# A hybrid decoder layer on one core: decay and rate products together, retention by alternating heads, all weight sums of the last two down parts by DMA, another order of the last products

## The chip, the cores and the metric

The kernel runs on one core of a Trainium2 chip. The time is that of one execution on the device, in microseconds (us). A core has a matrix engine (TensorE, PE in the profile), a vector engine (VectorE, DVE), a scalar engine (ScalarE, ACT), GpSimd (POOL), and SyncE (SP), which here does nothing but start DMA transfers. Each engine works off its own list of instructions in a fixed order; engines wait for each other by semaphores.

## What is computed

One layer of a decoder on 512 tokens of width 2048, all in float32. RMSNorm, a token mixer of four head groups that run side by side, an output projection, RMSNorm, an MLP with squared ReLU, a final RMSNorm:

```python
a = rmsnorm(x, norm1_w)
p_gdn, p_ret, p_m2, p_rw = split(a @ w_in)
o = concat([gated_deltanet(p_gdn), retention(p_ret), mamba2(p_m2), rwkv7(p_rw)])
h = x + o @ w_out
h = h + square(relu(rmsnorm(h, norm2_w) @ w_up)) @ w_down
out = rmsnorm(h, final_norm_w)
```

The change touches two of the head groups. Retention, per head and chunk, is `scores = (q k^T) * dmask`, `o = scores v + (q * qdec) R`, with a state `R` that is carried from chunk to chunk. RWKV-7 needs a decay, `exp(-exp(-softplus(-(w0 + tanh(wl) @ w_up)) - 0.5))`, and a rate, `a = sigmoid(a0 + al @ a_up)`; both come from small products with 32 rows.

## The kernel before

**Precision.** Each weight slab (128x1024) is split into a high part (`hi`, a cast on ACT) and a low part (`lo`, `raw - hi` on DVE); a product is three matmuls, hi by hi, hi by lo, lo by hi. Matmuls with plain float32 operands, as in the head groups, go through PE in two passes, and the trace lists each pass as a row.

**Token mixing.** `ORDER` lists 12 units: four of RWKV (`rwkv(j)`, "D"), four of gated DeltaNet ("A"), two of Mamba-2 ("C"), and last two of retention (`ret(j)`, "B"; each has two heads, `hh` = 0 and 1, in rows 0 to 63 and 64 to 127). Each unit first takes its parts of the input projection (`proj()`, line 457, 48 matmuls of 128x512 a part); the rest of a unit runs as a generator that is advanced by `tick()` once for every four matmuls of a later projection, so that its small matmuls lie between large ones. PE and POOL execute in exactly the order in which the code is written; the instructions of DVE, ACT and SP are put into an order by a scheduler when the kernel is built, and keep it. PSUM banks for small products come from a ring of six (`BK()`).

**MLP.** Both products of the MLP use Strassen-Winograd's scheme: seven products (numbered `m` = 1 to 7) in place of eight, with sums of weight blocks as operands. `up` runs from about 1076 to 1737 us, `down` from there to the end. `down` has eight parts `c`; each has two halves of columns `s`, in each the seven products in the order `DORD[c]`, and in each of them two slabs `i` (`dslab` counts the slabs) of 12 matmuls. `down_ahead` makes the splits of up to three slabs ahead of PE; there are four buffers each for `hi` and `lo`. Row blocks `t` = 0 and 1 have their results in `ht[t]`, those of tokens 256 to 511 in `ht[2 + t]`; a block of 128 tokens is finished by products 3, 2 (tokens 0 to 255) or 7, 4 (the others).

**Sums of weights.** Four of the seven weight operands in `down` are sums of blocks. Those of products 5 and 7 are made in DRAM beforehand: `add_weights` copies one block into a DRAM tile `t` by a DMA from POOL (line 313) and adds the other in an accumulating DMA one step later (lines 315, 318). A step is sent off by `add_one` after each of 52 projections, and after every seventh of the 216 products of `up` (`u % 7 == 4`); before each stands a `pace` copy on ACT and a multiplication on POOL. There were 64 steps. The sums of products 6 and 4 are made on DVE at the time of their split (line 1572), from the loaded sum of product 5 and the blocks of products 3 and 2 (`SUM`); `USES` says how many splits use a loaded slab.

**The end.** In part 7 each product is followed by the additions into `ht`; `finish` sends squares to ACT (line 377, summed along the row) and multiplies by the final norm's weights on DVE (line 1708); `write` takes the sum of squares to the power -0.5 on POOL (line 374), scales the four tiles of 128x512 of a row block (odd ones on ACT, line 1717, even ones on DVE, line 1719) and writes them out (line 1720).

Of the kernel before, what the change touches and what calls it, by code (L numbers as in the profile page):

```python
# [191 lines left out]
def tile_trunk(ctx: ExitStack, tc: tile.TileContext, ins, out):  # L192
# [104 lines left out]
        return ins["wdn"][4 * c + 2 * i + q, 2 * j + s]  # L297

    sums = {}

    def add_weights():

        late = None
        for c in range(8):
            for s in range(2):
                for q in range(2):
                    for m, y in ((5, wd(c, 0, 0, s, q)), (7, wd(c, 1, 1, s, q))):
                        h = yield
                        pace = cp.tile([128, 2], F32, tag="pace", name="pace", bufs=8)
                        A.copy(pace[:, 0:1], h[:, 0:1].bitcast(F32))  # L310
                        G.tensor_tensor(pace[:, 1:2], pace[:, 0:1], mhalf[:, 0:1], op=ALU.mult)  # L311
# [261 lines left out]
    def rwkv(j):  # L573
# [5 lines left out]

        bk = BK()  # L580
        PE.matmul(bk, lora[0:32, 512 + 128 * j:640 + 128 * j], m1[0:32], start=True, stop=True)
        sw = S("sw")
        A.activation(sw, bk, AF.Tanh, scale=0.5, bias=hb[:, j:j + 1])
        V.tensor_scalar(sw, sw, 1.0, None, op0=ALU.add)
        cs = S("cs")
        V.tensor_tensor_scan(cs, C("reset"), sw, 0.0, ALU.mult, ALU.add)
# [5 lines left out]
        V.tensor_copy(gc, gn[:, :, 63])  # L592
        k = shift((yield from proj()), Pm("mu", 4 + j), omu[:, 6 + j:7 + j])

        bk = BK()
        PE.matmul(bk, lora[96:128, cols], m0[96:128], start=True, stop=True)
        a = S("a")
        A.activation(a, bk, AF.Tanh, scale=0.5, bias=hb[:, 4 + j:5 + j])
        V.tensor_scalar(a, a, 0.5, 0.5, op0=ALU.mult, op1=ALU.add)
        kr = S("kr")  # L600
        V.tensor_scalar(kr, k, Pm("kk", j), None, op0=ALU.mult)
# [504 lines left out]
    def ret(j):  # L1106
        swap = [i ^ 1 for i in range(32)]

        def rot(acc):
            q = S("rq")  # L1110
            A.copy(q, acc)
            r = S("rr")
            V.tensor_tensor(r, q, C("cos"), op=ALU.mult)
            V.stream_shuffle(q, q, swap)
            V.tensor_tensor(q, q, C("sin"), op=ALU.mult)
            V.tensor_tensor(r, r, q, op=ALU.add)
            return r

        half = (slice(0, 64), slice(64, 128))
        qr = q4(rot((yield from proj())))  # L1120
        qd = q4(S("qd"))
        V.tensor_tensor(qd, qr, bc(C("qdec", 128 * j, 128).unsqueeze(1), (128, 4, 128)), op=ALU.mult)
        kf = rot((yield from proj()))
        kr = q4(kf)
        v0, v1 = S("rv0"), S("rv1")
        A.copy(v0, (yield from proj()))
        kd = S("kd").rearrange("p (c h d) -> p c h d", c=4, h=2)
        bk = tposes(None, kf)
        V.tensor_tensor(kd, bk.rearrange("p c (h d) -> p c h d", h=2),
                        bc(C("kdec", 2 * j, 2).unsqueeze(1).unsqueeze(3), (128, 4, 2, 64)), op=ALU.mult)  # L1130
        vt = [q4(S("vt0")), q4(S("vt1"))]
        PT = [q4(S("PT0")), q4(S("PT1"))]

        def scores(hh):
            bk = q4(BK())
            for c in range(4):
                PE.matmul(bk[:, c], kr[half[hh], c], qr[half[hh], c], start=True, stop=True)
            V.tensor_tensor(PT[hh], bk, bc(C("dmask", 128 * (2 * j + hh), 128).unsqueeze(1), (128, 4, 128)), op=ALU.mult)

        A.copy(v1, (yield from proj()))  # L1140
        tposes(vt[0], v0)
        scores(0)
        zg = [S("zg0"), S("zg1")]
        silu2(q4(zg[0]), (yield from proj()))
        tposes(vt[1], v1)
        scores(1)
        sb = q4(BK("sb"))
        R = q4(S("R"))
        for hh in range(2):
            for c in range(3):  # L1150
                PE.matmul(sb[half[hh], c], kd[:, c, hh], vt[hh][:, c], start=True, stop=True)
        V.tensor_copy(R[:, 0], sb[:, 0])
        for c in (1, 2):
            V.scalar_tensor_tensor(R[:, c], R[:, c - 1], C("rdec", j, 1), sb[:, c], op0=ALU.mult, op1=ALU.add)
        silu2(q4(zg[1]), (yield from proj()))
        yield "P"
        ocs = []
        for hh in range(2):
            ob = q4(BK("ob"))
            for c in range(4):  # L1160
                PE.matmul(ob[:, c], PT[hh][:, c], vt[hh][:, c], start=True, stop=c == 0)
                if c > 0:
                    PE.matmul(ob[:, c], qd[half[hh], c], R[half[hh], c - 1], start=False, stop=True)
            mu4, va, rs = small("mu4", 4), small("va", 4), small("rs", 4)
            V.tensor_reduce(mu4, ob, axis=AX.X, op=ALU.add)
            V.tensor_scalar(mu4, mu4, 1.0 / 128, None, op0=ALU.mult)
            oc = q4(S("oc"))
            V.tensor_tensor(oc, ob, bc(mu4.unsqueeze(2), (128, 4, 128)), op=ALU.subtract)
            sq = q4(S("sq"))
            A.activation(sq, oc, AF.Square)  # L1170
            V.tensor_reduce(va, sq, axis=AX.X, op=ALU.add)
            V.tensor_scalar(va, va, 1.0 / 128, EPS, op0=ALU.mult, op1=ALU.add)
            rsqrt(rs, va, 4)
            V.tensor_tensor(oc, oc, bc(rs.unsqueeze(2), (128, 4, 128)), op=ALU.mult)
            ocs.append(oc)
            yield 3
        yield 8
        for hh in range(2):
            bk = q4(BK())
            for c in range(4):  # L1180
                PE.transpose(bk[:, c], ocs[hh][:, c], ident)
            o = S("oB")
            V.scalar_tensor_tensor(q4(o), bk, hn[:, 1 + 2 * j + hh:2 + 2 * j + hh], q4(zg[hh]), op0=ALU.mult, op1=ALU.mult)
            keep_o(4 + 2 * j + hh, o)
# [310 lines left out]


    DPROD = {1: 2, 2: 1, 3: 0, 4: 4, 5: 6, 6: 7, 7: 5}
    DORD = [(1, 5, 6, 3, 2, 4, 7)] * 7 + [(1, 5, 6, 3, 2, 7, 4)]
    SUM = {6: (5, 3), 4: (5, 2)}
    USES = {1: 1, 5: 3, 3: 2, 2: 2, 7: 1}  # L1500
    dseq, dslab, dh, dop, dr = [], {}, {}, {}, {}
# [27 lines left out]
    def down_load():  # L1529

        if ds["l"] >= len(dseq):
            return False
        e = dseq[ds["l"]]
        if e[0] == "w":
            _, c, s, m, i = e
            m = SUM[m][1] if m in SUM else m
            e = ("w", c, s, m, i)
        if e in dr:
            ds["l"] += 1
            return True  # L1540
        n = len(homes["raw"])
        if len(ring) >= n and ring[-n][0] > 0:
            return False
        if e[0] == "x":
            src, uses = hq[e[1]][:, DPROD[e[2]]].rearrange("p k t -> p (k t)"), 1
        else:
            src = sums[m, c, s, i] if m in (5, 7) else wd(c, m != 1, m == 3, s, i)
            uses = USES[m]
        r = new_raw()
        nc.sync.dma_start(r, src)  # L1550
        dr[e] = [uses, r]
        ring.append(dr[e])
        ds["l"] += 1
        return True

    def down_ahead(i):

        while ds["s"] < len(dseq):
            e = dseq[ds["s"]]
            if e[0] == "w" and dslab[e[1:]] > i + 3:  # L1560
                break
            while ds["l"] <= ds["s"]:
                assert down_load()
            if e[0] == "x":
                both = AT("x").rearrange("p a t -> p (a t)")
                h, l = dop[e[1:]] = both[:, :1024], both[:, 1024:]
            else:
                h, l = dh[e[1:]] = new_halves()
            if e[0] == "w" and e[3] in SUM:
                _, c, s, m, q = e  # L1570
                r, other = (dr["w", c, s, x, q] for x in SUM[m])
                V.tensor_tensor(r[1], r[1], other[1], op=ALU.add)  # L1572
                other[0] -= 1
            else:
                r = dr[e]
            A.copy(h, r[1])  # L1576
            V.tensor_tensor(l, r[1], h.bitcast(F32), op=ALU.subtract)  # L1577
            r[0] -= 1
            ds["s"] += 1
        while ds["l"] < ds["s"] + 5 and down_load():  # L1580
            pass
# [128 lines left out]
    def write(t):  # L1710
# [2 lines left out]
        V.tensor_scalar(s1[:, 0:1], s1[:, 0:1], 1.0 / D, EPS, op0=ALU.mult, op1=ALU.add)  # L1713
        rsqrt(s1[:, 1:2], s1[:, 0:1], 1)
        for i in range(4):
            if i % 2:
                A.activation(ht[t][i], ht[t][i], AF.Copy, scale=s1[:, 1:2])
            else:
                V.tensor_scalar(ht[t][i], ht[t][i], s1[:, 1:2], None, op0=ALU.mult)
            (nc.sync, nc.scalar)[i % 2].dma_start(out[0, 128 * t:128 * t + 128, 512 * i:512 * i + 512], ht[t][i])  # L1720

    c = 7
# [49 lines left out]
```

## Time and profile before

| what | value |
|---|---|
| median of 3 runs | 2349.72 us (2349.24 to 2351.58) |
| the profiled execution, its own time | 2356.37 us |
| its span in the trace | 2354.6 us |
| mean granted PE clock | 0.992 |
| PE busy | 2290.2 us (97%) |
| DVE busy | 1772.2 us (75%) |
| ACT busy | 1016.7 us (43%) |
| POOL busy | 194.8 us (8%) |
| DMA | 404.76 MB, mean 172 GB/s |

Times in the trace are counted from the start of the span. PE is busy nearly all the time, so a stretch gets shorter where PE gets less to do or waits less. A row of the timeline has the start, the duration, the engine, the line, the operation, what it writes and reads, and in brackets the time that the engine stood idle before it and what ended that. Matmuls overlap, so what a run of them costs is read from start to start.

### The profile page before, as it was taken

What the parts mean: (1) busy time and instruction counts of PE and PEld (TensorE: products, weight loads), DVE (VectorE), ACT (ScalarE), POOL (GpSimd) and SP (SyncE); (2) the same over time, 40 slices, a digit from 0 to 9 for tenths busy, and PEclk for the clock granted to TensorE, in tenths of its full rate; (3) what the DMA queues carried; (4) which work ended last, traced back from release to release, by engine and by line L of the source; (5) the groups of instructions that cost most, each with busy time, mean ns of one, the idle gap of its engine ahead of it and who ended that gap; (6) DMA issues with size and microseconds to landing.
All of it is one profiled execution on the core that took longest, in us unless ns stands there. A gap on an engine that the chain in (4) does not pass through costs nothing.

```text
span 2354.6 us, 36711 instructions
## 1 busy us (share of the span) xinstructions
PE 2290.2 (97%) x14690; PEld 1969.7 (84%) x14690; DVE 1772.2 (75%) x2783; ACT 1016.7 (43%) x1480; POOL 194.8 (8%) x270
## 2 busy tenths in 40 slices
PE   6999999999999999998999999999999999999996
PEld 6777778878776788878999999999988888888885
DVE  5686855765684544469888888888888988898898
ACT  5323233333322232355455555555565444444443
POOL 1110211211111210011111000000010000000000
PEclk9999999999999999999999999999999999999998
DMA  5553625745553757565877754445486555656451
GB/s 201 148 144 90 170 78 147 182 123 143 153 153 95 196 151 243 154 227 175 243 221 206 218 172 137 158 157 169 149 312 199 196 185 163 215 172 213 157 192 72
DMA packets 159915, 404.76 MB, mean 172 GB/s; under 512 B 12928, under 2 KB 79488, under 8 KB 158720
## 3 DMA queue, kind: packets, MB, share of 16 engines
q1 hardware_dynamic: 83952, 285.42, 37.2%
q0 software_dynamic: 38912, 77.08, 14.5%
q10 hardware_dynamic: 36880, 39.92, 4.9%
q8 instruction: 115, 1.88, 0.3%
q14 instruction: 56, 0.46, 0.1%
HBM read 355.70 MB, written 113.77 MB: 199 GB/s over the span
## 4 chain that ended last, share of the span: by engine, by line
PE 78%; DVE 10%; issue 6%; DMA 4%; POOL 1%; ACT 1%; SPq 0%; POOLq 0%; DVEq 0%; ACTq 0%
PE acc L457 16%; PE p L1443 8%; PE p L1445 8%; PE p L1444 8%; PE dn L1677 8%; PE dn L1678 8%; PE dn L1676 8%; PE wo L1241 2%; PE wo L1242 2%; PE wo L1249 2%; DVE lo L282 1%; PE acc L481 1%; DMA h<-ct 1%; DVE lo L1577 1%; DVE xi L567 1%
## 5 line engine op out<-in xcount | busy, mean ns | idle before, releaser
L1576 ACT CAST hi<-raw 128x1024 fp32r<-128x1024 f32 x224 | 235.3, 1055 | 291.6 <-PE dn L1678 228.2
L1676 PE MATMUL dn<-hi,x 128*128 128x512 f32 x896 | 349.6, 390 | 5.6 <-ACT hi L1576 5.6
L1677 PE MATMUL dn<-lo,x 128*128 128x512 f32 x896 | 349.8, 390 | 3.2 <-DVE lo L1577 3.1
L1678 PE MATMUL dn<-hi,x 128*128 128x512 f32 x896 | 349.3, 390 | 0.0
L281 ACT CAST hi<-raw 128x1024 fp32r<-128x1024 f32 x162 | 169.7, 1049 | 401.6 <-PE acc L457 297.9
L457 PE MATMUL acc<-ah,hi 128*128 128x512 f32 x832 | 336.5, 404 | 0.0
L457 PE MATMUL acc<-al,hi 128*128 128x512 f32 x832 | 335.5, 403 | 0.0
L457 PE MATMUL acc<-ah,lo 128*128 128x512 f32 x832 | 333.8, 401 | 0.0
L1577 DVE TENSOR_TENSOR lo<-raw,hi 128x1024 fp32r<-128x1024 f32 x224 | 272.7, 1222 | 62.8 <-ACT hi L1576 62.4
L1436 ACT CAST hi<-raw 128x1024 fp32r<-128x1024 f32 x216 | 226.5, 1051 | 208.9 <-PE p L1444 149.3
L1437 DVE TENSOR_TENSOR lo<-raw,hi 128x1024 fp32r<-128x1024 f32 x216 | 262.7, 1221 | 70.7 <-ACT hi L1436 70.3
L282 DVE TENSOR_TENSOR lo<-raw,hi 128x1024 fp32r<-128x1024 f32 x160 | 195.2, 1222 | 141.1 <-ACT hi L281 124.9
L1676 PEld LDWEIGHTS dn<-hi,x 128*128 128x128 f32 x896 | 168.7, 188 | 41.5 <-ACT hi L1576 6.5
L1677 PEld LDWEIGHTS dn<-lo,x 128*128 128x128 f32 x896 | 168.6, 188 | 39.8 <-DVE lo L1577 4.9
L1678 PEld LDWEIGHTS dn<-hi,x 128*128 128x128 f32 x896 | 168.7, 188 | 34.8
L457 PEld LDWEIGHTS acc<-ah,hi 128*128 128x128 f32 x832 | 156.7, 188 | 38.5 <-issue 7.4
L457 PEld LDWEIGHTS acc<-ah,lo 128*128 128x128 f32 x832 | 156.7, 188 | 34.3 <-issue 2.9
L457 PEld LDWEIGHTS acc<-al,hi 128*128 128x128 f32 x832 | 156.9, 189 | 31.8 <-issue 1.9
L1434 DVE TENSOR_TENSOR raw<-raw,raw 128x1024 f32<-128x1024 f32 x124 | 151.4, 1221 | 2.2 <-DMA raw<-in_wup_dram 0.5
L1572 DVE TENSOR_TENSOR raw<-raw 128x1024 f32<-128x1024 f32 x64 | 77.7, 1221 | 0.6
L311 POOL TENSOR_TENSOR pace<-pace,mhalf 128x1 f32<-128x1 f32 x64 | 39.5, 618 | 443.6 <-ACT pace L310 443.6
L1445 PE MATMUL p<-s2h,lo 128*128 128x256 f32 x256 | 72.5, 283 | 0.8 <-DVE lo L1437 0.8
(500 smaller groups left out, 5008.0 us busy)
## 6 DMA issues: line engine op xcount, KB each, us to landing
raw<-in_wup_dram SPq DMA_DIRECT2D x136, 512.0 KB, 5.7
t<-in_wdn_dram POOLq DMA_DIRECT2D x128, 512.0 KB, 8.1
raw<-in_win_dram SPq DMA_DIRECT2D x106, 512.0 KB, 3.9
raw<-in_wdn_dram SPq DMA_DIRECT2D x96, 512.0 KB, 4.5
h<-ct ACTq DMA_DIRECT2D x32, 1024.0 KB, 10.1
raw<-t SPq DMA_DIRECT2D x64, 512.0 KB, 4.4
raw<-h SPq DMA_DIRECT2D x56, 512.0 KB, 4.3
raw<-in_wout_dram SPq DMA_DIRECT2D x48, 512.0 KB, 3.7
```

What stands on the lines that cost most here:

```text
L282: by.tensor_tensor(l[:, :w], r[:, :w], h[:, :w].bitcast(F32), op=ALU.subtract)
L457: PE.matmul(acc[:w], a, b, start=n == 0, stop=n == 47)
L1436: A.copy(h, r)
L1437: V.tensor_tensor(l, r, h.bitcast(F32), op=ALU.subtract)
L1443: PE.matmul(acc, wh, rh[:, k], start=k == 0, stop=False)
L1444: PE.matmul(acc, wh, rl[:, k], start=False, stop=False)
L1445: PE.matmul(acc, wl, rh[:, k], start=False, stop=k == 7)
L1576: A.copy(h, r[1])
L1577: V.tensor_tensor(l, r[1], h.bitcast(F32), op=ALU.subtract)
L1676: PE.matmul(accs[t], xh, h[:, ws], start=kk == 0, stop=False)
L1677: PE.matmul(accs[t], xh, l[:, ws], start=False, stop=False)
L1678: PE.matmul(accs[t], xl, h[:, ws], start=False, stop=kk == 3)
```

## The change

There are five edits.

1. In `rwkv`, the product for the rate stands right behind that for the decay, with its activation, instead of one projection later.
2. In `ret`, the scores of both heads are made in one go (`scores()`), head by head in turn, into two banks; the states alternate between the heads too, and so do the outputs, which had been one head after the other, with three ticks between.
3. `add_weights` also makes the sums of products 6 and 4 for parts 6 and 7 (`LATE = 6`): product 6 from a block and the sum of product 5, product 4 from a block and the sum of product 6. These are 16 more steps, 80 in all.
4. For those parts `down` loads one slab per product and does no additions on DVE.
5. In part 7 product 7 comes fourth instead of sixth, and `write` scales all tiles of row blocks 0 and 1 on ACT.

```diff
-                    for m, y in ((5, wd(c, 0, 0, s, q)), (7, wd(c, 1, 1, s, q))):
+                    parts = [(5, wd(c, 0, 1, s, q), wd(c, 0, 0, s, q)), (7, wd(c, 0, 1, s, q), wd(c, 1, 1, s, q))]
+                    if c >= LATE:
+                        parts += [(6, wd(c, 1, 1, s, q), 5), (4, wd(c, 1, 0, s, q), 6)]
+                    for m, x, y in parts:
...
-                        G.dma_start(d, wd(c, 0, 1, s, q))
+                        G.dma_start(d, x)
                         if late:
                             G.dma_start(*late, accum_op=ALU.add, max_dma_last_dim=1024)
-                        late = d, y
+                        late = d, (sums[y, c, s, q] if y in (5, 6) else y)
...
         PE.matmul(bk, lora[0:32, 512 + 128 * j:640 + 128 * j], m1[0:32], start=True, stop=True)
+        ba = BK()
+        PE.matmul(ba, lora[96:128, cols], m0[96:128], start=True, stop=True)
         sw = S("sw")
         A.activation(sw, bk, AF.Tanh, scale=0.5, bias=hb[:, j:j + 1])
+        a = S("a")
+        A.activation(a, ba, AF.Tanh, scale=0.5, bias=hb[:, 4 + j:5 + j])
...
-        bk = BK()
-        PE.matmul(bk, lora[96:128, cols], m0[96:128], start=True, stop=True)
-        a = S("a")
-        A.activation(a, bk, AF.Tanh, scale=0.5, bias=hb[:, 4 + j:5 + j])
...
-        def scores(hh):
-            bk = q4(BK())
+        def scores():
+            bks = [q4(BK()), q4(BK())]
             for c in range(4):
-                PE.matmul(bk[:, c], kr[half[hh], c], qr[half[hh], c], start=True, stop=True)
-            V.tensor_tensor(PT[hh], bk, bc(C("dmask", 128 * (2 * j + hh), 128).unsqueeze(1), (128, 4, 128)), op=ALU.mult)
+                for hh in range(2):
+                    PE.matmul(bks[hh][:, c], kr[half[hh], c], qr[half[hh], c], start=True, stop=True)
+            for hh in range(2):
+                V.tensor_tensor(PT[hh], bks[hh], bc(C("dmask", 128 * (2 * j + hh), 128).unsqueeze(1), (128, 4, 128)), op=ALU.mult)
...
-        for hh in range(2):
-            for c in range(3):
+        for c in range(3):
+            for hh in range(2):
                 PE.matmul(sb[half[hh], c], kd[:, c, hh], vt[hh][:, c], start=True, stop=True)
...
+        obs = [q4(BK("ob")), q4(BK("ob"))]
+        for c in range(4):
+            for hh in range(2):
+                PE.matmul(obs[hh][:, c], PT[hh][:, c], vt[hh][:, c], start=True, stop=c == 0)
+            for hh in range(2 if c > 0 else 0):
+                PE.matmul(obs[hh][:, c], qd[half[hh], c], R[half[hh], c - 1], start=False, stop=True)
         for hh in range(2):
-            ob = q4(BK("ob"))
-            for c in range(4):
-                PE.matmul(ob[:, c], PT[hh][:, c], vt[hh][:, c], start=True, stop=c == 0)
-                if c > 0:
-                    PE.matmul(ob[:, c], qd[half[hh], c], R[half[hh], c - 1], start=False, stop=True)
+            ob = obs[hh]
...
-    DORD = [(1, 5, 6, 3, 2, 4, 7)] * 7 + [(1, 5, 6, 3, 2, 7, 4)]
+    DORD = [(1, 5, 6, 3, 2, 4, 7)] * 7 + [(1, 5, 6, 7, 3, 2, 4)]
...
-            m = SUM[m][1] if m in SUM else m
+            m = SUM[m][1] if m in SUM and c < LATE else m
...
-            src = sums[m, c, s, i] if m in (5, 7) else wd(c, m != 1, m == 3, s, i)
-            uses = USES[m]
+            src = sums[m, c, s, i] if (m, c, s, i) in sums else wd(c, m != 1, m == 3, s, i)
+            uses = USES[m] if c < LATE else 1
...
-            if e[0] == "w" and e[3] in SUM:
+            if e[0] == "w" and e[3] in SUM and e[1] < LATE:
...
-            if i % 2:
+            if i % 2 or t < 2:
                 A.activation(ht[t][i], ht[t][i], AF.Copy, scale=s1[:, 1:2])
```

What this makes of the lists of instructions is shown at three places. The first is PE's list in the first retention unit, from the transposes of `v1` on (`rv`), with `vt`, `PT` and the state `R` as above. Before:

```order
L1004 MATMUL bk<-ident,rv_7171 128x128 x4
L1137 MATMUL bk<-rr 128x128 x4
L1151 MATMUL sb<-vt_7388,kd 64x128 x3
L1151 MATMUL sb<-vt_7389,kd 64x128 x3
```

and, one projection later, the outputs of its first head:

```order
L1161 MATMUL ob<-vt_7388,PT_7390 128x128 x2
L1163 MATMUL ob<-R,qd 128x128
L1161 MATMUL ob<-vt_7388,PT_7390 128x128
L1163 MATMUL ob<-R,qd 128x128
L1161 MATMUL ob<-vt_7388,PT_7390 128x128
L1163 MATMUL ob<-R,qd 128x128
```

Now the scores of both heads stand one projection earlier, and the outputs of both heads in one block:

```order
L1166 MATMUL ob<-vt_7388,PT_7390 128x128
L1166 MATMUL ob<-vt_7389,PT_7391 128x128
L1166 MATMUL ob<-vt_7388,PT_7390 128x128
L1166 MATMUL ob<-vt_7389,PT_7391 128x128
L1168 MATMUL ob<-R,qd 128x128 x2
L1166 MATMUL ob<-vt_7388,PT_7390 128x128
L1166 MATMUL ob<-vt_7389,PT_7391 128x128
L1168 MATMUL ob<-R,qd 128x128 x2
```

The second block of the other head, three ticks later, is gone, and consecutive matmuls are now of different heads.

The second place is the end of ACT's list. The tiles are named after the column block, `h_1` is the second, and a number: before, 17645 to 17648 are row block 0, the next four row block 1, then 2, then 3. Before, the last rows were these:

```order
L1576 CAST hi<-raw 128x1024
L377 ACTIVATE junk,fss<-h_3_17656 128x512
L377 ACTIVATE junk,fss<-h_3_17660 128x512
L377 ACTIVATE junk,fss<-h_1_17654 128x512
L377 ACTIVATE junk,fss<-h_1_17658 128x512
L1717 ACTIVATE h_1_17654<-h_1_17654,s_22443 128x512
L1717 ACTIVATE h_3_17656<-h_3_17656,s_22443 128x512
```

Now 17741 to 17744 are row block 0, and so on, and the end of ACT's list reads (between the fences two more scalings and the issues of writes are left out):

```order
L381 ACTIVATE junk,fss<-h_1_17750 128x512
L1724 ACTIVATE h_0_17741<-h_0_17741,s_22497 128x512
L1724 ACTIVATE h_1_17742<-h_1_17742,s_22497 128x512
L1724 ACTIVATE h_2_17743<-h_2_17743,s_22497 128x512
```

```order
L1724 ACTIVATE h_3_17748<-h_3_17748,s_22513 128x512
L1724 ACTIVATE h_1_17750<-h_1_17750,s_22555 128x512
L1727 DMA out_dram<-h_3_17748 128x512
L1727 DMA out_dram<-h_1_17750 128x512
L1724 ACTIVATE h_3_17752<-h_3_17752,s_22555 128x512
L381 ACTIVATE junk,fss<-h_1_17754 128x512
```

The square of the last tile of row block 3 (`h_1_17754`) now stands behind the eight scalings of row blocks 0 and 1 and two of row block 2; before, all squares stood ahead of the scalings of row blocks 2 and 3, and one cast stood behind the scalings of row blocks 0 and 1.

The third place is DVE's list at the end. Now (`fw` are the final norm's weights, `s` the scale of a row block):

```order
L1687 TENSOR_TENSOR h_1_17742<-h_1_17742,dn 128x512
L1687 TENSOR_TENSOR h_1_17746<-h_1_17746,dn 128x512
L1687 TENSOR_TENSOR h_1_17750<-h_1_17750,dn 128x512
L1715 TENSOR_TENSOR h_1_17742<-h_1_17742,fw 128x512
L1719 TENSOR_REDUCE s_22497<-fss 128x1
L1715 TENSOR_TENSOR h_1_17746<-h_1_17746,fw 128x512
L1720 TENSOR_SCALAR s_22497<-s_22497 128x1
```

Before, the last sum of a weight slab and the scalings of row blocks 0 and 1 stood ahead of product 7's additions:

```order
L1572 TENSOR_TENSOR raw<-raw 128x1024
L1719 TENSOR_SCALAR h_0_17645<-h_0_17645,s_22340 128x512
L1719 TENSOR_SCALAR h_2_17647<-h_2_17647,s_22340 128x512
L1713 TENSOR_SCALAR s_22356<-s_22356 128x1
L1680 TENSOR_TENSOR m_17643<-m_17643,dn 128x512
```

The sums of slabs are gone from DVE's list, and the addition from the last product (`h_1_17750`, row block 2) now stands ahead of the first scale of row block 0.

More of the change, by code (lines that the diff above doesn't have):

```diff
@@ L299, in tile_trunk @@
     sums = {}
+    LATE = 6
     def add_weights():
@@ L1132, in ret @@
         PT = [q4(S("PT0")), q4(S("PT1"))]
-        def scores(hh):
-            bk = q4(BK())
+        def scores():
+            bks = [q4(BK()), q4(BK())]
             for c in range(4):
-                PE.matmul(bk[:, c], kr[half[hh], c], qr[half[hh], c], start=True, stop=True)
-            V.tensor_tensor(PT[hh], bk, bc(C("dmask", 128 * (2 * j + hh), 128).unsqueeze(1), (128, 4, 128)), op=ALU.mult)
+                for hh in range(2):
+                    PE.matmul(bks[hh][:, c], kr[half[hh], c], qr[half[hh], c], start=True, stop=True)
+            for hh in range(2):
+                V.tensor_tensor(PT[hh], bks[hh], bc(C("dmask", 128 * (2 * j + hh), 128).unsqueeze(1), (128, 4, 128)), op=ALU.mult)
         A.copy(v1, (yield from proj()))
         tposes(vt[0], v0)
-        scores(0)
+        scores()
         zg = [S("zg0"), S("zg1")]
@@ L1145, in ret @@
         tposes(vt[1], v1)
-        scores(1)
         sb = q4(BK("sb"))
         R = q4(S("R"))
-        for hh in range(2):
-            for c in range(3):
+        for c in range(3):
+            for hh in range(2):
                 PE.matmul(sb[half[hh], c], kd[:, c, hh], vt[hh][:, c], start=True, stop=True)
```

## The prediction

> **What bounds the kernel now.** I read the busy times by stretch first (start and end, length, then busy us of PE, PEld, DVE, ACT, POOL with counts, granted clock, DMA share, GB/s).
>
> ```profile
> 64.00:760.00 696.00, 685.93 (x4893) 531.65 (x4892) 473.40 (x1226) 222.42 (x415) 105.98 (x139) 1.00 0.53 136
> 1170.00:1400.00 230.00, 230.00 (x1931) 230.00 (x1932) 192.84 (x232) 124.22 (x182) 20.71 (x28) 1.00 0.70 209
> 1400.00:1737.00 337.00, 337.00 (x2769) 334.39 (x2768) 278.08 (x336) 183.09 (x258) 0.00 (x0) 1.00 0.49 162
> 2127.00:2203.00 76.00, 76.00 (x337) 62.96 (x336) 66.67 (x71) 35.26 (x34) 0.00 (x0) 1.00 0.57 187
> 2260.00:2300.00 40.00, 40.00 (x178) 33.15 (x177) 39.70 (x53) 18.39 (x29) 0.00 (x0) 1.00 0.37 120
> 2300.00:2344.00 44.00, 35.88 (x144) 27.62 (x142) 41.38 (x61) 18.16 (x30) 2.08 (x2) 0.92 0.13 48
> ```
>
> PE has no idle time in `up` and in nearly all of `down`: there only less PE work would help, and the change takes none. In the last 44 us PE is busy for 35.88 while DVE is full from 2260 on: the end of part 7 is bound by DVE. So two places can gain: small matmuls in the token mixing, and the end.
>
> **The rate's product.** The timeline of PE around the decay's product (`m,lora`, 32 rows) in the first unit:
>
> ```profile
> 64.75 0.39 PE L457 MATMUL acc<-ah,lo 128*128 128x512 f32 x1
> 65.07 1.12 PE L581 MATMUL bk<-m,lora 32*128 32x512 f32 x2
> 66.12 0.50 PE L457 MATMUL acc<-ah,hi 128*128 128x512 f32 x1
> 66.46 0.40 PE L457 MATMUL acc<-al,hi 128*128 128x512 f32 x1
> 66.69 0.39 PE L457 MATMUL acc<-ah,lo 128*128 128x512 f32 x1
> ```
>
> Three large matmuls in a row take 3 x 0.227 = 0.68 us from start to start (last rows: 0.23 each). Here 66.69 - 64.75 = 1.94, so the two passes cost 1.26: about 0.85 for the passes and 0.4 for the change of shape before and after. The rate's product costs the same 13 us later. Put behind the decay's, it uses rows 96 to 127 of the array, which the other leaves free, and another bank. Whether such neighbours run at once shows in the same shapes elsewhere:
>
> ```profile
> 104.05 1.16 PE L664 MATMUL bk<-AR,KB 64*128 64x128 f32 x16
> 105.14 0.50 PE L457 MATMUL acc<-ah,lo 128*128 128x512 f32 x1
> ...
> 777.79 1.16 PE L1137 MATMUL bk<-rr 64*128 64x128 f32 x8
> 778.87 1.15 PE L1151 MATMUL sb<-vt,kd 128*64 128x128 f32 x12
> 779.95 0.50 PE L457 MATMUL acc<-ah,hi 128*128 128x512 f32 x1
> ```
>
> Line 664 alternates between row halves and banks and needs 1.09 us for 16 passes; retention's scores, of the same shape but all in one half, need 1.08 for 8. Neighbours in different rows and banks run at once. With quarters I expect the same: the four units save 4 x 1.26 = **5.0 us**. If they did not overlap, only the changes of shape would go, 4 x 0.4 = 1.6; that is the lower end, and 5.0 the upper. I take 5.0, nearest to line 664.
>
> **Retention, per unit.** Scores: 16 passes in turn cost what 8 did (1.09), so the second block of 1.08 goes, with some 0.1 for its change of shape: 1.2. States: 12 passes took 1.08 (above) to 1.2; they lie in different column halves, and line 750 shows those overlapping too:
>
> ```profile
> 185.94 0.34 PE L750 MATMUL sb<-VX,KT 128*64 128x64 f32 x4
> 186.11 0.29 PE L758 MATMUL yb<-VX,Ph 128*64 128x64 f32 x4
> ```
>
> Four passes in 0.17. Line 1151's passes, of 128 columns, come to 1.08 / 12 = 0.09 each head after head; with line 750's pace, 0.04 for half as many columns, they would stay at 0.09, and with full overlap, as in line 664's 1.09 / 16 = 0.07, twelve take 0.8. I take 0.3 saved (0 to 0.5). Outputs, one head:
>
> ```profile
> 791.87 0.60 PE L1161 MATMUL ob<-vt,PT 128*128 128x128 f32 x4
> 792.40 0.49 PE L1163 MATMUL ob<-R,qd 64*128 64x128 f32 x2
> 792.82 0.49 PE L1161 MATMUL ob<-vt,PT 128*128 128x128 f32 x2
> ...
> 794.48 0.50 PE L457 MATMUL acc<-al,hi 128*128 128x512 f32 x1
> ```
>
> One head takes 794.48 - 791.87 = 2.61, and the large matmul behind it 0.11 more (as at 66.12: 0.34 to the next instead of 0.23): 2.72, twice 5.44. Each turn from 128 rows to 64 or back makes two passes cost 0.42 instead of 0.22. In one block: eight `PT` passes, 0.9; three pairs of `R` at once, 3 x 0.42; twice four `PT` passes behind a turn, 2 x 0.63; the way out, 0.2: 3.6. Saved 1.85. A unit saves 1.2 + 0.3 + 1.85 = 3.35, two **6.7 us**; 3 if only the changes of shape went.
>
> Against that stands one wait. In the first unit DVE waits 6.2 us for the mask, and PE behind it 4.4:
>
> ```profile
> 765.55 0.69 DVE L1138 TENSOR_TENSOR PT<-bk,dmask 128x512 f32<-128x512 f32 x1 [6.22 <-DMA dmask<-in_wide_dram]
> 766.56 0.80 PE L978 MATMUL yb<-Yc,QT 128*128 128x128 f32 x2 [4.39 <-DVE Yc L966]
> ```
>
> Two masked products now stand ahead of `Yc`, for which PE waits: **+0.6 us**. The token mixing gains 5.0 + 6.7 - 0.6 = **11.1** (4 to 12). Between 64 and 760 us PE is busy for 685.93 of 696, so a shorter list ends sooner.
>
> **Sixteen more sums.** They fall into the stretch from 1400, which had none; each is a small copy on ACT, a small step on POOL and two DMAs of 0.5 MB. In the stretch from 1170 there were nine (28 rows on POOL, three a step), the DMA share was 0.70 instead of 0.49, and PE waited for nothing. So I take 0; the price if that cover fails stands with the rivals. In `down`, parts 6 and 7 load 28 slabs of 0.5 MB each instead of 20. That is one in 2.72 us of PE (12 x 0.227), 193 GB/s, where the row from 2127 shows 187 at a share of 0.57: 0 too. DVE loses 16 additions of 1.14; in part 6 PE did not wait for it, so this counts in part 7 alone.
>
> **The end: what goes.** PE's waits in the last half:
>
> ```profile
> 2308.06 0.40 PE L1678 MATMUL dn<-hi,x 128*128 128x512 f32 x1
> 2309.04 0.51 PE L1676 MATMUL dn<-hi,x 128*128 128x512 f32 x1 [0.58 <-ACT hi L1576]
> 2310.30 0.51 PE L1677 MATMUL dn<-lo,x 128*128 128x512 f32 x1 [0.76 <-DVE lo L1577]
> ...
> 2331.72 0.39 PE L1678 MATMUL dn<-hi,x 128*128 128x512 f32 x1
> 2337.14 0.80 PE L1676 MATMUL dn<-hi,x 128*128 128x512 f32 x1 [5.03 <-ACT hi L1576]
> 2339.42 0.79 PE L1677 MATMUL dn<-lo,x 128*128 128x512 f32 x1 [1.49 <-DVE lo L1577]
> ...
> 2343.49 0.39 PE L1678 MATMUL dn<-hi,x 128*128 128x512 f32 x1
> ```
>
> From 2331.72 to 2343.49 there are 12 steps, 2.72 us at full pace, which took 11.77: 9.05 lost (part of it at half the clock after the wait). From 2308.06 to 2310.30 two steps took 2.24 instead of 0.45, 1.8 lost, with 0.1 behind. Together 11.0. Does it all go? DVE's work per product, by these two rows:
>
> ```profile
> 2309.02 2.36 DVE L1577 TENSOR_TENSOR lo<-raw,hi 128x1024 fp32r<-128x1024 f32 x2
> 2311.30 2.49 DVE L1680 TENSOR_TENSOR h<-h,m 128x512 f32<-128x512 f32 x4
> ```
>
> A `lo` 1.14, an addition 0.60. Products 1, 5, 6, 7, 3, 2, 4 then take 4.7, 5.9, 5.9, 8.3, 4.7, 4.7, 4.7 = 38.9 us of DVE against 7 x 5.44 = 38.1 of PE; before, with four more sums, 43.5. After product 7 DVE is 24.8 - 21.8 = 3 us behind, and what follows lets it catch up; the splits run up to three slabs, 8.2 us, ahead. So I expect PE to wait for nothing or for about 1 us, and its last matmul, at E, comes **11.0 us** earlier (10 to 11).
>
> **The end: what comes.** Before, E was 2343.9 and the span ended 10.7 us later. Now row blocks 0 and 1 are finished by the product before the last, and DVE's and ACT's lists decide. These rows have the prices:
>
> ```profile
> 2330.45 1.53 POOL L374 TENSOR_TENSOR s<-s,mhalf 128x1 f32<-128x1 f32 x1 [71.74 <-DVE s L1712]
> 2345.54 1.01 POOL L374 TENSOR_TENSOR s<-s,mhalf 128x1 f32<-128x1 f32 x1 [11.96 <-DVE s L1713]
> ...
> 2344.70 0.63 ACT L377 ACTIVATE junk<-h 128x512 f32<-128x512 f32 x1 [1.23 <-DVE h L1680]
> 2346.59 1.33 ACT L1717 ACTIVATE h<-h,s 128x512 f32<-128x512 f32 x2 [1.17 <-POOL s L374]
> ...
> 2348.00:2350.00 2.00, 0.00 (x0) 0.00 (x0) 0.88 (x2) 1.33 (x2) 0.35 (x1) 0.50 1.06 406
> 2352.00:2354.60 2.60, 0.00 (x0) 0.00 (x0) 0.00 (x0) 0.00 (x0) 0.00 (x0) 0.50 0.46 175
> ```
>
> DVE makes the last product's first addition at E - 1.4 (six matmuls before the end), and only then the multiplication, the sum and the scale for row block 0: E + 0.7. POOL, 1.5: E + 2.3. ACT: eight scalings of 0.66 for row blocks 0 and 1, two for row block 2 and the issue of a write between, 7.0: E + 9.3. Only then the last square, 0.7: E + 10.0. DVE's multiplication, sum and scale for row block 3, 1.0; POOL 1.0: E + 12.1. From a first scaling to the end it was 2354.6 - 2346.59 = 8.0 before, of which 5.2 went to writing 2.1 MB at 406 GB/s; now 1.05 MB are left, 2.6: 5.4. The end is at **E + 17.5**, 6.8 later than before (5 to 8). The end gains 11.0 - 6.8 = **4.2** (2 to 6).
>
> [...]
>
> **Sum.** 11.1 + 4.2 = 15.3. The traced execution took 2356.37 by its own time, 1.8 more than its span; less 15.3 that is 2341.1. The median of before is 6.65 lower; on its scale the time is 2349.72 - 15.3 = **2334.4 us**, and the bounds of all terms (4 + 2 to 12 + 6) give 2332 to 2344.
>
> **Rivals.**
> *The small matmuls do not overlap* as rows of other shapes suggest, or units wait for DVE a little later instead: the mixing gains its lower end, 4 to 7; total 8 to 11, 2339 to 2342. For it: DVE has its own list, and a chain of small steps that waits for it swallows time won on PE. Against: line 664 alternates in just this way.
> *The end gives everything back.* If ACT's list costs 4 us more after E, or DVE lets PE wait once more, the end gains 0: 2338.6. It speaks for it that the list of ACT puts a square behind ten scalings; if the writes of row blocks 0 to 2, 3.1 MB or 7.7 us at 406 GB/s, were still running at E + 12.1, that would cost as much; they should be done at about E + 11.6.
> *The end is better*: POOL and ACT a little quicker, 2 to 4 us more: 2330 to 2332.
> *The sums hold up `up`* (slower). Nine steps raised the DMA share by 0.21 over 230 us, 48 us or 5.4 us of all 16 engines each; 16 more are 86. If weight loads queued behind them and PE waited for all of it, the time would be 2334 + 86 = 2420; it is slower than before by 0.2% from 15.3 + 4.7 = 20 us on, a quarter of that. Against it: with these steps running, PE was busy 230.00 of 230.
> [...] The page of the profile has their mean:
>
> ```profile
> L311 POOL TENSOR_TENSOR pace<-pace,mhalf 128x1 f32<-128x1 f32 x64 | 39.5, 618 | 443.6 <-ACT pace L310 443.6
> ```
>
> [...]
> *The change does nothing that can be measured*: gains of the mixing lost to waits and the end at 0: 2346 to 2350.
>
> **Chances.** Forecast, 2330.5 to 2338: 0.62. Less overlap, 2338 to 2342: 0.17. The end gives more back, 2338 to 2341: 0.08. Better, below 2330.5: 0.06. No change: 0.04. Slower: 0.03. A measurement of this kernel tells 0.2% (4.7 us) from no change; so faster 0.93, same 0.04, slower 0.03. The range leaves out the last two cases and little of the others: 2328.5 to 2343.
>
> **What would show it.** Right: `lora` passes as one group of four rows in about 1.1 us; scores 16 passes in about 1.1; outputs in 3.6; no PE wait over 1 us after 2250; a tail of 17 us behind the last matmul, with ACT's last square about 10 us after it; PE busy throughout `up` with a DMA share near 0.7. Wrong: passes of different heads that start 0.1 us apart, PE waits for DVE in the head groups that were not there, PE waits for `hi` in part 7 (a cast held up behind a square), or waits for `raw` in `up`.

## The result and the profile after

The changed kernel takes **2337.26 us** (median of 4 runs, 2334.78 to 2340.51), the kernel before took 2350.65 beside it (4 runs, 2349.24 to 2354.54): a ratio of **0.994**, 95% interval 0.9928 to 0.9951, or 13.4 us less. The forecast of 2334.4 against 2349.72 is a ratio of 0.9935 and lies in that interval; on the clock the result is 2.9 us later than forecast, of which 0.9 is the higher median of before beside it, and the saving is 13.4 us instead of 15.3.

The profiled execution took 2336.49 us by its own time with a span of 2334.7. That span is 19.9 shorter than the one of before, more than the medians differ: the traced execution of before was 6.65 above its median. So I compare stages and not spans. From the page of the changed kernel, first the busy times of the engines, then groups:

```profile
span 2334.7 us, 36812 instructions
...
PE 2275.5 (97%) x14690; PEld 1962.8 (84%) x14690; DVE 1751.5 (75%) x2763; ACT 1021.1 (44%) x1500; POOL 228.6 (10%) x318
...
DMA packets 171180, 429.94 MB, mean 184 GB/s; under 512 B 13696, under 2 KB 88448, under 8 KB 169728
...
L1684 PE MATMUL dn<-lo,x 128*128 128x512 f32 x896 | 348.8, 389 | 0.0
...
L315 POOL TENSOR_TENSOR pace<-pace,mhalf 128x1 f32<-128x1 f32 x80 | 50.5, 631 | 724.0 <-ACT pace L314 717.7
```

The 16 further sums are there (80 steps on POOL instead of 64), and the matmuls of `down` wait for nothing (idle before them, the last column, 0.0). The busy times by stretch, with the columns as before; the last four match the prediction's rows from 1400, 2127, 2260 and 2300, the last three shifted by what the kernel has gained up to there:

```profile
64.00:760.00 696.00, 684.77 (x4916) 533.46 (x4914) 474.36 (x1233) 221.90 (x415) 107.80 (x140) 1.00 0.53 137
...
1400.00:1737.00 337.00, 337.00 (x2717) 332.12 (x2716) 278.64 (x333) 185.77 (x269) 35.18 (x53) 1.00 0.69 211
2110.00:2186.00 76.00, 76.00 (x337) 62.93 (x336) 62.84 (x67) 36.03 (x35) 0.00 (x0) 1.00 0.65 214
2242.00:2282.00 40.00, 40.00 (x178) 33.14 (x177) 37.34 (x50) 19.65 (x27) 2.12 (x4) 1.00 0.65 216
2282.00:2318.30 36.30, 36.27 (x160) 29.69 (x159) 35.83 (x52) 16.28 (x28) 0.00 (x0) 1.00 0.12 40
```

In the second half of `up` the DMA share rose from 0.49 to 0.69 and PE is still busy for 337.00 of 337. At the end PE runs through to its last matmul (36.27 of 36.30, before 35.88 of 44).

The rate's product, in the timeline of PE:

```profile
66.17 0.39 PE L461 MATMUL acc<-ah,lo 128*128 128x512 f32 x1
66.49 0.69 PE L585 MATMUL bk<-m,lora 32*128 32x512 f32 x1
66.50 0.69 PE L587 MATMUL bk<-m,lora 32*128 32x512 f32 x1
67.03 0.59 PE L585 MATMUL bk<-m,lora 32*128 32x512 f32 x1
67.03 0.59 PE L587 MATMUL bk<-m,lora 32*128 32x512 f32 x1
67.55 0.50 PE L461 MATMUL acc<-ah,hi 128*128 128x512 f32 x1
67.89 0.40 PE L461 MATMUL acc<-al,hi 128*128 128x512 f32 x1
68.12 0.39 PE L461 MATMUL acc<-ah,lo 128*128 128x512 f32 x1
```

From `ah,lo` to the next `ah,lo` it is 68.12 - 66.17 = 1.95 us; before, with half of the passes, it was 1.94. Four passes cost what two did.

Retention's first unit, also PE's timeline:

```profile
761.40 0.66 PE L982 MATMUL yb<-Yc,QT 128*128 128x128 f32 x2 [2.75 <-DVE Yc L970]
...
772.30 0.60 PE L1008 MATMUL bk<-ident,rv 128*128 128x128 f32 x4
772.83 0.43 PE L1156 MATMUL sb<-vt,kd 128*64 128x128 f32 x2
773.90 0.87 PE L1156 MATMUL sb<-vt,kd 128*64 128x128 f32 x10 [0.64 <-ACT vt L1010]
774.70 0.50 PE L461 MATMUL acc<-ah,hi 128*128 128x512 f32 x1
...
786.62 1.05 PE L1166 MATMUL ob<-vt,PT 128*128 128x128 f32 x8
787.60 0.49 PE L1168 MATMUL ob<-R,qd 64*128 64x128 f32 x4
788.02 0.71 PE L1166 MATMUL ob<-vt,PT 128*128 128x128 f32 x4
788.66 0.49 PE L1168 MATMUL ob<-R,qd 64*128 64x128 f32 x4
789.09 0.71 PE L1166 MATMUL ob<-vt,PT 128*128 128x128 f32 x4
789.73 0.49 PE L1168 MATMUL ob<-R,qd 64*128 64x128 f32 x4
```

The outputs take about 3.6 us, as expected. New is a wait in the states: the second pair of passes (head 1) waits for ACT's copy of `vt[1]` out of PSUM. Before, the scores of head 1 stood between the transposes (`ident,rv`) and the states and covered that copy; now nothing does. ACT's copy, before (PE's scores of head 1 ran from 777.79 to 778.87, the states followed) and now:

```profile
778.23 0.58 ACT L1006 COPY vt<-bk 128x512 f32<-128x512 f32 x1
```

```profile
773.27 0.58 ACT L1010 COPY vt<-bk 128x512 f32<-128x512 f32 x1
```

The end, in the timeline of all engines; `s` on POOL is the scale of a row block, `junk` the square of a tile:

```profile
2317.88 0.39 PE L1685 MATMUL dn<-hi,x 128*128 128x512 f32 x1
2318.15 0.15 DVE L1719 TENSOR_REDUCE s<-fss 128x1 f32<-128x4 f32 x1
...
2319.05 2.04 POOL L378 TENSOR_TENSOR s<-s,mhalf 128x1 f32<-128x1 f32 x3 [74.53 <-DVE s L1719]
...
2320.08 1.95 ACT L1724 ACTIVATE h<-h,s 128x512 f32<-128x512 f32 x3 [1.64 <-POOL s L378]
...
2326.91 0.61 ACT L381 ACTIVATE junk<-h 128x512 f32<-128x512 f32 x1
...
2327.65 0.69 DVE L1715 TENSOR_TENSOR h<-h,fw 128x512 f32<-128x512 f32 x1 [5.64 <-ACT junk L381]
...
2328.68 0.55 POOL L378 TENSOR_TENSOR s<-s,mhalf 128x1 f32<-128x1 f32 x1 [7.59 <-DVE s L1720]
2329.26 1.33 ACT L1724 ACTIVATE h<-h,s 128x512 f32<-128x512 f32 x2 [1.64 <-POOL s L378]
```

The last matmul ends at E = 2317.88 + 0.39 = 2318.3, the span 16.4 us later. DVE sits idle for 5.64 us because the last square stands in ACT's queue behind ten scalings.

### The profile page after: what moved, and what is told of

Its sections match the earlier page's. It is cut to its first block, busy times and chain, and to the rows that moved or that the text cites. A ratio compares the mean times of both kernels' runs of the same rounds, so it can differ in the third digit from the quotient of the medians.

```text
span 2334.7 us, 36812 instructions
## 1 busy us (share of the span) xinstructions
PE 2275.5 (97%) x14690; PEld 1962.8 (84%) x14690; DVE 1751.5 (75%) x2763; ACT 1021.1 (44%) x1500; POOL 228.6 (10%) x318
## 4 chain that ended last, share of the span: by engine, by line
PE 83%; DVE 8%; issue 6%; DMA 1%; POOL 1%; ACT 1%; SPq 0%; POOLq 0%; DVEq 0%; ACTq 0%
PE acc L461 16%; PE p L1450 9%; PE p L1451 9%; PE p L1452 9%; PE dn L1684 9%; PE dn L1683 9%; PE dn L1685 9%; PE wo L1248 2%; PE wo L1249 2%; PE wo L1256 2%; DVE lo L282 1%; PE acc L485 1%; DVE xi L571 1%; DVE cv L807 1%; DVE xm L572 1%
## 5 line engine op out<-in xcount | busy, mean ns | idle before, releaser
L315 POOL TENSOR_TENSOR pace<-pace,mhalf 128x1 f32<-128x1 f32 x80 | 50.5, 631 | 724.0 <-ACT pace L314 717.7
L1451 PE MATMUL p<-s2l,hi 128*128 128x256 f32 x256 | 72.5, 283 | 0.0
```

Of the source, the lines that this page charges most:

```text
L1451: PE.matmul(acc, wh, rl[:, k], start=False, stop=False)
```

## The experiments

Each ratio is to the kernel before on the same chip, with its 95% interval. The edits are numbered as in the section on the change. "Excess" is what a stretch of 20 large matmuls of the projections takes from start to start beyond 20 x 0.2268 us, their pace there; the stretches are counted alike in all kernels.

### One part at a time: the rate (edit 1)

```diff
+        ba = BK()
+        PE.matmul(ba, lora[96:128, cols], m0[96:128], start=True, stop=True)
...
-        bk = BK()
-        PE.matmul(bk, lora[96:128, cols], m0[96:128], start=True, stop=True)
```

> Only the rate's product moved behind the decay's (edit 1). If the two run at once, as in the trace of the changed kernel, four units save 4 x 1.26 = 5.0 us: ratio 0.9979. If only the changes of shape went: 1.6 us, 0.9993.

Measured: 2346.01 us, ratio **0.9978** (0.997 to 0.9987), 5.2 us less. In the trace the four stretches that held the second product have 1.21 to 1.27 us less excess; one stretch with a merged pair has 0.1 more, so it is 4.9 in all. The passes overlap nearly in full.

### The heads (edit 2)

```diff
-        def scores(hh):
+        def scores():
...
-        scores(0)
+        scores()
...
-        scores(1)
...
+        obs = [q4(BK("ob")), q4(BK("ob"))]
```

> Only retention's heads interleaved (edit 2). By the recorded sum: scores 2 x 1.2, states 2 x 0.3, outputs 2 x 1.85, less 0.6 for the mask: 6.1 us saved, ratio 0.9974. The rival, from the trace of the changed kernel: with the second block of scores gone the states wait for the copy of vt on ACT, so scores and states bring nothing and only the outputs' 3.7 us remain: 0.9984; PE then shows a wait of 0.6 to 1.1 us ahead of the states in both units.

Measured: 2348.31 us, ratio **0.9984** (0.9975 to 0.9992), 3.8 us less. The sum on record (0.9974) stands just outside the interval, the rival in its middle. The waits of PE up to 900 us carry it:

```profile
PE yb L978 <- DVE Yc L966: 3.0, 2, 2.8
...
PE sb L1152 <- ACT vt L1006: 1.7, 2, 1.1
```

(in total, times, the longest.) The second wait, 0.64 and 1.08 us, is not in the trace of before.

### The sums alone (edits 3 and 4)

```diff
+    LATE = 6
...
+                    if c >= LATE:
+                        parts += [(6, wd(c, 1, 1, s, q), 5), (4, wd(c, 1, 0, s, q), 6)]
...
-            if e[0] == "w" and e[3] in SUM:
+            if e[0] == "w" and e[3] in SUM and e[1] < LATE:
```

> Only the sums in DRAM for parts 6 and 7, with their loads (edits 3 and 4); the old order at the end and the old scaling. If the sums on DVE were what made PE wait, PE's 11 us of waits at the end go, and the tail behind the last matmul stays about 11 to 12 us: 10 us saved, ratio 0.996. If the old order makes PE wait by itself (scalings ahead of the last cast and split), 5 us of the wait stay and no more than 5 us are saved. If the added steps hold up the products of up, PE waits between 1400 and 1740.

Measured: 2344.36 us, ratio **0.9965** (0.9953 to 0.9977), 8.2 us less. From 2240 us to its end PE waits for nothing. The second half of part 7, from the 841st of the 896 steps of `down` to E, takes 38.24 us; before it took 49.67, and the changed kernel takes 38.24 too. So the sums alone bring the whole 11.4 us. The tail behind E grows from 10.71 to 14.24, more than the 11 to 12 expected, since PE no longer waits for DVE and so ends while DVE still has product 7's additions in front of it.

### The order alone (edit 5)

```diff
-    DORD = [(1, 5, 6, 3, 2, 4, 7)] * 7 + [(1, 5, 6, 3, 2, 7, 4)]
+    DORD = [(1, 5, 6, 3, 2, 4, 7)] * 7 + [(1, 5, 6, 7, 3, 2, 4)]
...
-            if i % 2:
+            if i % 2 or t < 2:
```

> Only the last order and the scaling on ACT (edit 5), the sums of products 6 and 4 still on DVE. DVE then has 43.5 us of work for 38.1 of PE, so PE still waits for DVE by 2 to 6 us, in products 6 to 4, but no longer behind scalings; the tail behind the last matmul grows from 10.7 to about 16.5. Theory: waits down by 5 to 9, tail up by 6: between 3 saved and 1 lost, ratio 0.9987 to 1.0004. Rival: the order alone takes the waits away, 5 us saved, 0.998.

Measured: 2352.82 us, ratio **1.0003** (0.9994 to 1.0011): nothing. PE's waits from 2240 us on, 5.8 us:

```profile
PE dn L1677 <- DVE lo L1577: 5.1, 5, 1.6
PE dn L1676 <- ACT hi L1576: 0.7, 1, 0.7
```

The second half of part 7 takes 44.35 us instead of 49.67 and the tail 14.53 instead of 10.71: a gain of 5.3, of which 3.8 is given back. The 1.5 that are left lie at the edge of the interval.

### The cover for the copy

In the changed kernel the scores of both heads go behind the transposes of `vt[1]`:

```diff
-        scores()
...
         tposes(vt[1], v1)
+        scores()
```

> The changed kernel, but the scores of both heads stand behind the transposes of v1, so that they cover the copy of vt again. Theory (the states wait for the copy of vt on ACT because the scores no longer lie between): PE's waits of 0.64 and 1.08 us ahead of the states go, and the scores' 2.2 us lie in their place as cover; against the kernel before scores and states now gain 2.5 to 3 us in all, so 2335.5, 1.5 to 2.5 us better than the changed kernel, ratio to before 0.9932. Rival (the wait comes from DVE or from the mask): PE waits as long elsewhere, no gain, 0.994; the mask's DMA now starts later, and if DVE waits for it ahead of two splits, PE loses 2 to 4 us.

Measured: 2329.94 us, ratio **0.9907** (0.9893 to 0.992): 7.3 us less than the changed kernel, by the medians. Both waits for `vt` are gone. PE's timeline of this kernel:

```profile
763.28 0.60 PE L1008 MATMUL bk<-ident,rv 128*128 128x128 f32 x4
763.82 1.16 PE L1142 MATMUL bk<-rr 64*128 64x128 f32 x16
764.91 0.88 PE L1156 MATMUL sb<-vt,kd 128*64 128x128 f32 x12
765.71 0.50 PE L461 MATMUL acc<-ah,hi 128*128 128x512 f32 x1
```

All 16 scores in 1.09 us and all 12 states in 0.80, the 0.3 less that the prediction took for them. A change of shape ahead of the scores is gone too. The gain is more than was expected, since another wait has gone with it: PE's 2.75 us for `Yc`. By the excess, the stages edited are 7.1 us shorter than in the changed kernel: 2.5 of it is the block of scores ahead of the copy (1.3 in each unit; the scores now lie where the waits for `vt` were), 4.6 the wait for `Yc` and its aftermath. DVE still waits for the mask:

```profile
771.61 1.29 DVE L1144 TENSOR_TENSOR PT<-bk,dmask 128x512 f32<-128x512 f32 x2 [5.64 <-DMA dmask<-in_wide_dram]
```

but `Yc` is now ahead of it on DVE, and PE has enough to do until `PT` is read.

### The mask issued early

That reading has its own test: the place of the changed kernel, with the mask's load issued at the start of the unit.

```diff
+        C("dmask")
         qr = q4(rot((yield from proj())))
```

> The changed kernel with the load of the mask dmask issued at the start of each retention unit instead of at its first use; nothing else is moved. Theory: PE's wait ahead of yb<-Yc,QT near 761 us (2.75 us in the changed kernel's trace) and the two us at half clock behind it are the mask's price, and the early issue takes them away: 4 to 5 us less than the changed kernel, ratio about 0.992. The waits of sb for the copy of vt (0.64 and 1.08 us) stay. Rival: the load lands late because the queue ahead of it is long, not because it is issued late: the wait stays above 2 us and the ratio at 0.994.

Measured: 2332.89 us, ratio **0.9924** (0.9911 to 0.9936), 4.4 us less than the changed kernel by the medians, 3.8 by the ratios. The intervals of the two ratios (0.9928 to 0.9951 for the changed kernel) overlap a little, so the size rests on the trace. PE's waits from 700 to 900 us:

```profile
PE sb L1157 <- ACT vt L1010: 1.7, 2, 1.1
```

The wait for `Yc` is gone, the one for `vt` stays. The excess of the two stretches around it falls from 6.52 + 2.89 to 3.41 + 1.46 us: 4.5.

### The place without the overlap

The kernel before, with one line moved:

```diff
-        scores(0)
         zg = [S("zg0"), S("zg1")]
...
         tposes(vt[1], v1)
+        scores(0)
         scores(1)
```

> The kernel before with one line moved: the scores of head 0 are computed right ahead of those of head 1, behind the transposes of vt[1]; the passes of the heads are not interleaved, and nothing of the rest is changed. It separates the place from the overlap. Theory: by its place alone PE's wait for the mask near 766 us (4.39 us in the trace of before) goes, as in e5_cover, where no PE work stood behind the waiting product, with the time at half clock behind it: 5 to 6 us less, ratio about 0.9976. Rival: the later product with the mask holds up the states behind it on DVE, or the scores of the first head were filling a wait of PE for the first transposes: no gain, ratio 0.9995 or above.

Measured: 2346.52 us, ratio **0.9979** (0.997 to 0.9988), 5.6 us less by the medians, from a move of four matmuls and one product. DVE's product waits for the mask (7.14 us, at 780.68), PE's wait is gone. PE's timeline tells what the overlap itself is worth:

```profile
771.39 1.71 PE L1137 MATMUL bk<-rr 64*128 64x128 f32 x16
773.03 1.14 PE L1151 MATMUL sb<-vt,kd 128*64 128x128 f32 x12
```

Scores 1.64 us against 1.09 with the heads in turn. Two separate blocks of eight took 1.08 each, so of what the scores save in a unit about half comes from having one block instead of two, and half from the turns.

### The sharing of the last scalings

The changed kernel with the old sharing, and the order as changed:

```diff
-            if i % 2 or t < 2:
+            if i % 2:
```

> The changed kernel with the old scaling: row blocks 0 and 1 half on ACT, half on DVE. If ACT's eight scalings ahead of the last square make the tail, it gets four scalings shorter, 2.6 us: tail 13.8 instead of 16.4, ratio to before 0.993. If the writes bound it (4.2 MB at 406 GB/s are 10.3 us), it gets shorter by 1 us at most.

Measured: 2338.18 us, ratio **0.9951** (0.9937 to 0.9965), tail 16.04 instead of 16.45. A miss. ACT's timeline:

```profile
2326.91 1.63 ACTq L1727 DMA_DIRECT2D out_dram<-h  x2
2328.58 0.63 ACT L381 ACTIVATE junk<-h 128x512 f32<-128x512 f32 x1 [1.09 <-issue]
```

Six scalings instead of ten do not help the last square, since ACT then waits for POOL's scales (1.64, 0.42 and 0.90 us) and issues writes between them (1.09 us of idle time ahead of the square). It is the order that puts them ahead of the square, whoever does them.

### The old order in the changed kernel

Edit 5 is undone, the rest kept.

```diff
-    DORD = [(1, 5, 6, 3, 2, 4, 7)] * 7 + [(1, 5, 6, 7, 3, 2, 4)]
+    DORD = [(1, 5, 6, 3, 2, 4, 7)] * 7 + [(1, 5, 6, 3, 2, 7, 4)]
...
-            if i % 2 or t < 2:
+            if i % 2:
```

> The changed kernel without edit 5: old last order, old scaling. By the run with the sums alone (tail 14.2, no waits of PE) it ends 2.2 us earlier than the changed kernel: 2335, ratio 0.993. If the new order is needed to keep PE from waiting, it is slower than the changed kernel by 1 us or more.

Measured: 2335.48 us, ratio 0.9936 (0.9924 to 0.9949), as expected. The second half of part 7 takes 38.24 us with either order, and the tail is 14.24 instead of 16.45. With the sums in DRAM the new order wins no time of PE and costs 2.2 us behind it; the timing alone doesn't tell 0.9936 from 0.994.

### Two more last orders

First the changed kernel with the last order (1, 5, 6, 7, 4, 3, 2) and the old sharing:

```diff
-    DORD = [(1, 5, 6, 3, 2, 4, 7)] * 7 + [(1, 5, 6, 7, 3, 2, 4)]
+    DORD = [(1, 5, 6, 3, 2, 4, 7)] * 7 + [(1, 5, 6, 7, 4, 3, 2)]
```

> The changed kernel with the last order 1, 5, 6, 7, 4, 3, 2 and the old scaling: row blocks 2 and 3 are finished two products before the end, and their 2.1 MB are written while PE works; only row blocks 0 and 1 remain behind the last matmul. Tail 11 to 12 us instead of 16.4, PE waits below 1 us: 4.5 to 5.5 us better than the changed kernel, 2332.5, ratio 0.992. Rival: DVE is then 4 us behind at product 4, and PE waits 2 us or more for the last splits.

Measured: 2335.13 us, ratio 0.9936 (0.9923 to 0.995), tail 13.94: half of what was hoped for. The last squares no longer stand behind scalings (the last scaling group starts at E + 5.9 instead of E + 11.0), but two row blocks instead of one are left to be scaled and written then, 8.0 us instead of 5.4.

Then this order and sharing and the covered copy together, the two edits shown above:

> The changed kernel with the scores of both heads computed behind the transposes of vt[1] instead of ahead of them (as in e5_cover), with the last order 1, 5, 6, 7, 4, 3, 2 and with the old sharing of the last scalings (as in e8_7432). Theory: the two gains lie in different stages and add. The ratio of e5_cover was 0.9907; the tail behind the last matmul was 16.45 us in the changed kernel and 13.94 in e8_7432, with no wait of PE in part 7 in either, so 2.5 us more go: ratio 0.9897, about 2327 us, tail about 14 us. Rival: the place of the scores gives only a draw of the mask's waiting time, and the end's other half an us of load: then the ratio stays at 0.9905 or above.

Measured: 2330.27 us, ratio 0.9911 (0.9895 to 0.9926). The tail is 13.94, as expected, but the time is that of the covered copy alone (0.9907, 0.9893 to 0.992). In the trace E comes 4.6 us later than there, of it 2.1 at the start of the span and the rest between 860 and 1800 us, outside of the edited stages. Whether the 2.5 us of the tail reach the time stays open. Both kernels beat the changed one.

## Why the prediction came out as it did

The saving was 13.4 us where 15.3 was forecast, and the sign and most of the terms were right too. Behind that stand one term that failed, two at the end that paid more, and several that held. That the total is so near is in part luck: by the terms below the token mixing gained 8.2 us instead of 11.1, and the end 5.7 instead of 4.2. The parts as measured in the traces:

| term | predicted | measured |
|---|---|---|
| rate's product | -5.0 | -4.9 (alone -5.2 by time) |
| outputs, two units | -3.7 | -3.7 (excess 5.52 to 3.68, 5.54 to 3.68) |
| scores and states, two units | -3.0 | -0.3 |
| second product ahead of `Yc` | +0.6 | +0.7 at the same landing of the mask |
| sums in `up`, loads in `down` | 0 | 0 |
| E in part 7 | -11.0 | -11.4 |
| tail | +6.8 | +5.7 |
| sum | -15.3 | -13.9; by time -13.4 |

**Where it failed: "the second block of 1.08 goes ... 1.2. States ... I take 0.3 saved".** As a count of PE's passes this was nearly right: with the scores behind the transposes, as tried above, the block ahead of them goes (1.3 us in each unit) and the excess around the states falls by another 0.26 in the first unit and 0.0 in the second. But the step asked only what the block cost, not what it covered. Removed from behind the transposes, it uncovered ACT's copy of `vt[1]`, and PE waited 0.64 and 1.08 us. In the second unit the block of 16 passes ahead costs what that of 8 did (1.26 and 1.25), and the excess around the states is 2.84 before and 2.84 after: the whole saving went into the wait. In the first unit 0.3 was left of it. The prediction named such a case as a rival ("units wait for DVE a little later instead"), but looked for it on DVE; it came from ACT. A smaller point: no row shows the split of the rate's 1.26 us into 0.85 for the passes and 0.4 for the change of shape. From start to start the two passes take 1.05 and the edges add 0.2, so the lower end would have been 0.8 instead of 1.6; since the passes overlapped, nothing hung on it.

**The mask.** The mechanism of the +0.6 held, but the wait as a whole didn't grow: it fell from 4.39 to 2.75 in this pair of traces. The 0.7 shows when the wait is set against the mask's time from issue to landing. These are traces of nine kernels of this study, four with the scores as before and five with those of the changed kernel:

```
place       landing, us              PE's wait, us                  landing - wait
before      9.0, 7.6, 7.1, 6.9       4.39, 3.01, 2.48, 2.30         4.59 to 4.62
changed     6.7, 6.7, 6.7, 6.6, 6.4  2.75, 2.76, 2.79, 2.74, 2.46   3.86 to 3.95
```

PE waits for the landing less 4.6 us before, less 3.9 in the changed kernel: 0.7 more, one masked product. What varies is the landing, and all five of the changed kernel's are shorter than all four of before, so that the mean wait is 2.70 us against 3.05; why they are shorter no run shows. So in these traces the term cost nothing net, and that is luck as far as the prediction goes. The cheaper step was to look at this wait not as something to be lengthened by 0.6 but as 4 to 5 us to be had, as the traces of the early issue and of the other place then showed.

**The end.** PE's waits went as forecast, and no `hi` or `lo` came late. In the tail the steps came at E + 1.8 (first scalings; forecast 2.3), E + 8.6 (the start of the last square; 9.3), E + 11.0 (scaling of row block 3; 12.1) and E + 16.4 (17.5). The chain was the right one. POOL's last step was half as long as assumed (0.55 instead of 1.0), and the path from E to the first scaling was 0.5 shorter. What the prediction did not see is that edit 5 isn't needed for the gain: it took "before, with four more sums, 43.5" of DVE's work against 38.9 after, and did not ask whether the old order, with 38.9 as well, would do. It does, with 2.2 us less of a tail.

**The sums.** The rival in which they hold up `up` is refuted by the row from 1400: busy in full at a DMA share of 0.69, with 0.7 expected. POOL's small step took 631 ns on average instead of 618; no other engine waited for it.

Of the rivals, "the small matmuls do not overlap" fell with the first experiment; its other half, waits a little later, is what happened to scores and states. "The end gives everything back" fell with the traces: 5.7 of 11.4.

## What to carry over

When a block of work is taken from the bound engine, ask what it was covering: what ran on other engines while it ran, and who reads that next. Merge blocks at the later place, where their operands are long there and they still hide the next copy; here the later place was worth 7.3 us beside the 13.4 of the whole change, about 2.5 of it by this and the rest because the wait for the mask went too. And when a wait ends at a load, look at when the load is issued before counting what the wait will be: one line that issued it earlier was worth about 4 us (4.4 by the medians, 4.5 in the trace).

## What the runs showed of the hardware

**After waits of nearly the same length PE's clock dropped or it didn't.** Two of the kernels waited 2.75 us (the changed one, to 761.40) and 2.79 us (last order 1, 5, 6, 7, 4, 3, 2, to 760.13) for `Yc`. The windows right behind, first of the changed kernel (the granted clock is the third number from the end):

```profile
761.40:763.00 1.60, 1.60 (x5) 1.41 (x6) 0.29 (x1) 0.51 (x1) 0.00 (x0) 0.53 0.01 5
763.00:765.00 2.00, 2.00 (x6) 1.37 (x5) 0.85 (x2) 0.12 (x1) 0.87 (x1) 0.52 0.00 0
```

and of the other:

```profile
760.00:763.00 3.00, 2.87 (x32) 2.29 (x34) 1.14 (x3) 1.39 (x2) 0.35 (x1) 1.00 0.01 4
```

At 0.53 the large matmuls step at 0.43 us instead of 0.23 (762.29 to 762.72 in the changed kernel). In the other traces they kept their pace after waits of 2.30 and 2.76 us and fell to half of it after 2.46, 2.48, 2.74, 3.01 and 4.39. The price in the changed kernel was 1.6 us: an excess of 6.52 + 2.89 against 6.42 + 1.40 in the kernel with edit 2 alone, which waited 2.76 and kept its clock. How long the clock stayed at half: 3.4 us in three of the traces, those of before (windows of 0.5 us from 766.0 to 769.5), of the changed kernel (from 761.5 to 765.0) and of edit 5 alone (worked out from 0.73 and 0.71 in its windows from 764 to 767 and from 767 to 770); in that of the old order in the changed kernel, which waited 2.74, the clock was 0.50 in both windows from 761 to 764 and from 764 to 767. No run shows what decides whether it drops.

**The rate's passes started together with the decay's.** Their operands lie in rows 96 to 127 and 0 to 31. The two products start 0.01 us apart, and the second costs next to nothing (1.95 us instead of 1.94 in the rows above). In the unrounded trace of the changed kernel it is 6 to 8 ns in all eight pairs of passes. Turns between 128 and 64 rows kept their price per turn: four `R` passes of both heads take 788.02 - 787.60 = 0.42 us, as two of one head did before (from 792.40 to 792.82).
